# Attention with queries scaled by 1/rms at their layout and the output divided by the sum of the softmax weights

## The chip, the core and the metric

One core of a Trainium2 chip runs the whole program. Its engines work side by side, each through its own queue in order: TensorE (PE, with its weight loads PEld), VectorE (DVE), ScalarE (ACT), GpSimd (POOL), and SyncE (SP), which issues the transfers. The metric is the device time of one execution in microseconds.

## The reference

Two layers of an encoder on 512 tokens of width 1024. Each layer has a mixer, in which attention and a state space part (SSD) share one input and one output projection, and then a feed-forward part (SwiGLU). What matters here is the attention: 8 query heads of 64 and 2 key heads, queries and keys divided by their root mean square (rms) and rotated by position, then, per block of 128 queries, softmax and the weighted sum of the values:

```python
q = rms_norm(q.reshape(b, l, N_Q_HEADS, HEAD_DIM), q_norm_w[i]).astype(jnp.float32)
k = rms_norm(k.reshape(b, l, N_KV_HEADS, HEAD_DIM), k_norm_w[i]).astype(jnp.float32)
...
    def one_block(qi):
        s = jnp.einsum("bqgrd,bkgd->bgrqk", qi, k)
        p = jax.nn.softmax(s, axis=-1)
        return jnp.einsum("bgrqk,bkgd->bqgrd", p, v)
...
    mixed = jnp.concatenate([attn_out, ssd_out], axis=-1)
    x = x + jnp.einsum("ble,ed->bld", mixed, w_out[i])
```

Softmax: with m the largest score of a row, the weights are exp(s - m), divided by their sum.

## The kernel before

Activations lie with features on the partitions, 8 tiles of 128x512; weights come in chunks of 128x1024 floats. Each weight is split into a high and a low part (`whi`, cast on ACT, L188; `wlo`, subtracted on DVE or GpSimd, L189), and so is each operand (`xh`, `xl`); a product is three matmuls (`mm3`, L407 to L409; `mm3a`, L415 to L417).

The mixer of a layer weaves three generators together (`drain`, L926): `fill` (input projections of queries, of x/B/C with their convolution, of z, and then the first half of the output projection), `ssd` (the scan in chunks of 128 tokens) and `att` (attention). A scheduler then sets the order of the instructions on each engine, so that the order in the program is not the one written.

Attention works on 8 blocks, 4 query blocks c for each of 2 key heads g, with 4 query heads j each: 32 pairs of head and block in a layer, 64 in all. `queries` (L646) lays a block out: it copies the 4 heads twice side by side (`qd`, ACT), transposes them on PE and splits them (`qh`, `ql`). `attention` (L659) then does, for each head:

- two matmuls, queries against keys, into the scores `s_` (L664, L665);
- the negated maximum `nm` of each row (L667, DVE), times the query's 1/rms `ri` (L668, DVE);
- `p_` = exp(ri * s_ + nm) with the row sums in `sm` (L670, ACT);
- 1/sm (L671, DVE) and `p_` times it (L675, DVE, 128x512);
- four transposes of `p_` (L678, PE), a copy to SBUF (`t_ring`, ACT);
- after each second head, the product with the values (L688, PE) and the copy of the 128x128 output into `qr` (L690, ACT), in place of the queries.

So the queries are rotated but not divided by their rms when they are laid out: the 1/rms (`qri`, worked out by `rsqrt` on DVE from the sums of squares) comes in at the exponential. The weights are divided before they are used.

At the end of `fill`, `out_half(1, ...)` multiplies the SSD half of the output projection: 8 tiles m of 12 matmuls, each added to `part` (L791, DVE). Then, for j = 0 to 3 (two heads each), the attention's output is split into `mixed.h[j]` (L850, ACT) and `mixed.l[j]` (L851, recorded as xl<-qr,xh L94, DVE). After `drain`, `out_half(0, ...)` multiplies the attention half; its tile m needs all four j. The two halves are called half 1 and half 0 below, in this order of time.

In the SSD part, `chunk` adds the product `yd` to `y` (L766, DVE) before PE may go on to the product with the state (L771); `finish` works out the 1/rms of the SSD half (`yri`) and multiplies `xs` by it (L891).

Of the kernel before, what the change touches and what calls it, by code (L numbers as in the profile page):

```python
# [15 lines left out]
F32 = mybir.dt.float32  # L16
F32R = mybir.dt.float32r
I32 = mybir.dt.int32
AF = mybir.ActivationFunctionType
ALU = mybir.AluOpType  # L20
# [3 lines left out]
P = 128  # L24
# [4 lines left out]
NC = S // P  # L29
# [6 lines left out]
PRODUCTS = "11 c1 c2 22 t3 21 c4".split()  # L36
SRAW = 6

NORM = "VVVV"
PTE = "AAAA"  # L40
GGE = "GG"
QDE, OUTE, _, YE, HE, WE, RAE, MLE, DSE = "AAVGVGVVG"
EB, GGB = 2, 4
DDW, DDE = 512, "A"
MORE = "VGGVG"
# [24 lines left out]
def merge(a, b, c):  # L70
    return a.rearrange("p (b c) -> p b c", b=b, c=c)


def bc(ap, shape, axis):
    return ap.unsqueeze(axis).broadcast_to(shape)
# [3 lines left out]
def tile_hybrid_encoder(ctx, tc, xt_d, par_d, rope_d, snw_d, w_kvdt, w_xbc, w_q, w_z, w_out, w_gate, w_up, w_down, out_d):  # L79
    nc = tc.nc  # L80
    V, A, G, T = nc.vector, nc.scalar, nc.gpsimd, nc.tensor
# [8 lines left out]
    def copy(e, out, in_):  # L90
        A.copy(out, in_) if e == "A" else (G if e == "G" else V).tensor_copy(out, in_)

    def tt(e, *args):
        (G if e == "G" else V).tensor_tensor(*args)  # L94

    def bank(tag):


        return psum.tile([P, S], F32, name=f"ps_{tag}", tag=tag)
# [148 lines left out]
    ident = const.tile([P, P], F32, name="ident")  # L248
# [193 lines left out]
    def mixer(l, norm, mx):  # L442
# [21 lines left out]
        base = mx.tile([P, 2, NC, 64], F32, name="base", tag="t2", bufs=B2)  # L464
# [29 lines left out]
        if l == 0:  # L494
            for t, rows, v in ((segr, (0, 32), 1.0), (segl, (64, 72), -1.0)):
                G.memset(t.bitcast(F32), 0.0)
                for r in rows:
                    G.affine_select(out=t, in_=t.bitcast(F32), pattern=[[-1, 8], [0, P]], compare_op=ALU.not_equal, fill=v,
                                    base=-r, channel_multiplier=1)
# [3 lines left out]
        for d in range(2):  # L503
            for r in (0, 32):
                V.tensor_copy(acw[:, d, :, r:r + 8], ac[:, :, 8 * d:8 * d + 8])
            p_ = bank("m")
            for c in range(NC):
                T.matmul(p_[:64, c * P:(c + 1) * P], lhsT=acw[:, d, c], rhs=mask[("le", "ge")[d]], start=True, stop=True)
            for r in (0, 32):
                dst, src = segl[r:r + 8, 4 * d:4 * d + 4], merge(p_[r:r + 8], NC, P)  # L510
# [50 lines left out]
        for g in range(2):  # L561
            p_ = bank("m")
# [47 lines left out]
        qr = mx.tile([P, NC, 8, 64], F32, name="qr")  # L610
# [17 lines left out]
        qri = {}  # L628
# [13 lines left out]
        def ring(which):  # L642
            turn[which] += 1
            return rings[which][:, turn[which] % 4]

        def queries(c, g):  # L646

            qd = mx.tile([P, 4, 2, 64], F32, name="qd", tag="qd")
            copy(QDE, qd, bc(qr[:, c, 4 * g:4 * g + 4], [P, 4, 2, 64], 2))
            tp = bank("t")  # L650
            for j in range(4):
                T.transpose(tp[:, j * P:(j + 1) * P], qd[:, j].rearrange("p a d -> p (a d)"), ident)
            qh = mx.tile([P, S], F32R, name="qh", tag="qh", bufs=2)
            ql = mx.tile([P, S], F32R, name="ql", tag="ql", bufs=2)
            A.copy(qh, tp)
            V.tensor_tensor(ql, tp, qh.bitcast(F32), ALU.subtract)
            return qh, ql

        def attention(c, g, qh, ql):  # L659
            nm = mx.tile([P, 4], F32, name="nm", tag="nm", bufs=2)  # L660
            sm = mx.tile([P, 4], F32, name="sm", tag="sm", bufs=2)
            for j in range(4):
                s_ = bank("s")
                T.matmul(s_, lhsT=qh[:, j * P:(j + 1) * P], rhs=KK[:, g], start=True, stop=False)  # L664
                T.matmul(s_, lhsT=ql[:, j * P:(j + 1) * P], rhs=KK[:, g], start=False, stop=True)  # L665
                ri = qri[g][:, c, j:j + 1]
                V.tensor_reduce(nm[:, j:j + 1], s_, AX.X, ALU.max, negate=True)  # L667
                V.tensor_tensor(nm[:, j:j + 1], nm[:, j:j + 1], ri, ALU.mult)  # L668
                p_ = ring("p")
                A.activation(p_, s_, AF.Exp, bias=nm[:, j:j + 1], scale=ri, accum_out=sm[:, j:j + 1])  # L670
                V.reciprocal(sm[:, j:j + 1], sm[:, j:j + 1])  # L671
                if NORM[j] == "A":
                    A.activation(p_, p_, AF.Copy, scale=sm[:, j:j + 1])
                else:
                    (G if NORM[j] == "G" else V).tensor_scalar(p_, p_, sm[:, j:j + 1], None, ALU.mult)  # L675
                t_ = bank("t")
                for kt in range(NC):
                    T.transpose(t_[:, kt * P:(kt + 1) * P], p_[:, kt * P:(kt + 1) * P], ident)  # L678
                pt = merge(ring("t"), NC, P)
                copy(PTE[j], pt, merge(t_, NC, P))  # L680
                if j % 2 == 0:
                    first = pt
                    continue
                o_ = bank(O_BANK)

                for kt in range(NC):
                    for e, t2 in enumerate((first, pt)):
                        T.matmul(o_[64 * e:64 * e + 64, :P], lhsT=Vt[:, kt, g * 64:(g + 1) * 64],  # L688
                                 rhs=t2[:, kt], start=kt == 0, stop=kt == NC - 1)
                copy(OUTE, qr[:, c, 4 * g + j - 1:4 * g + j + 1].rearrange("p h d -> p (h d)"), o_[:, :P])  # L690
                yield
# [126 lines left out]
        def fill():  # L818
# [25 lines left out]
            yield from out_half(1, range(KT), part, part)  # L844
            while "att" not in done:
                yield
            for j in range(4):
                src = qr.rearrange("p c (j a) d -> p j c (a d)", a=2)[:, j]
                h = mixed.h[j].rearrange("p (c q) -> p c q", c=NC)
                A.copy(h, src)  # L850
                tt(MLE, mixed.l[j].rearrange("p (c q) -> p c q", c=NC), src, h.bitcast(F32), ALU.subtract)  # L851
            Z["part"] = part

        def drain(*gens):
# [309 lines left out]
```

## Time and profile before

| | us |
|---|---|
| three runs | 1280.83, 1285.01, 1288.04 |
| median | 1285.01 |
| the profiled execution, its own time | 1282.91 |
| its span in the profile | 1281.2 |
| PE, DVE, ACT, POOL busy | 1212.7, 953.1, 618.5, 265.6 |
| mean granted clock of TensorE | 0.977 |

Read it so: PE is busy for nearly the whole span, but matmuls are pipelined, so a busy PE is not one at its peak. The mixers lie at about 20 to 265 us and 645 to 885 us; between and after them is the feed-forward part. Shares over the span mix stages with different limits, so the stages of a mixer are read one by one.

### The profile page before, as it was taken

The numbers are of one execution on the slowest core, as the hardware profiler recorded it, in microseconds if no ns is written. First come the engines' busy times: TensorE is split into PE (matmuls) and PEld (weight loads), VectorE is DVE, ScalarE is ACT, GpSimd is POOL, SyncE is SP. The second block draws the span as 40 slices with busy tenths as digits, with TensorE's granted clock in tenths as the row PEclk, the third lists the DMA queues.
The fourth block names the chain that finished last, engine by engine and source line by source line (L and its number), as shares of the span: only waits on it lengthen the run. The fifth ranks groups of instructions, "written<-read, shape, count | busy, mean of one in ns | idle before, by whom it ended". The sixth has DMA issues, their size and how long they took to land.

```text
span 1281.2 us, 19691 instructions
## 1 busy us (share of the span) xinstructions
PE 1212.7 (95%) x7694; PEld 1072.8 (84%) x7694; DVE 953.1 (74%) x1561; ACT 618.5 (48%) x1131; POOL 265.6 (21%) x208
## 2 busy tenths in 40 slices
PE   6898998999799999999998999899988999999996
PEld 6777887687798999899897787778878889989995
DVE  7899889666874687567679989985597458845853
ACT  4556655543442354244455575754354324523544
POOL 6423655010400000000134255420022000000002
PEclk8999998999899999999999999989999999999998
DMA  5221022125133133221442211112502422332122
GB/s 175 94 71 50 34 67 75 33 93 170 50 116 99 66 129 119 74 71 42 128 141 88 66 34 66 59 34 83 197 17 93 138 72 94 124 119 72 40 61 79
DMA packets 45229, 110.04 MB, mean 86 GB/s; under 512 B 5168, under 2 KB 5680, under 8 KB 45136
## 3 DMA queue, kind: packets, MB, share of 16 engines
q1 hardware_dynamic: 45136, 108.79, 26.4%
q8 instruction: 60, 0.98, 0.3%
q14 instruction: 33, 0.27, 0.1%
HBM read 104.44 MB, written 4.33 MB: 85 GB/s over the span
## 4 chain that ended last, share of the span: by engine, by line
PE 70%; DVE 21%; issue 3%; ACT 2%; POOL 2%; DMA 1%; DVEq 0%; ACTq 0%; POOLq 0%
PE ps_a L1025 5%; PE ps_a L1026 5%; PE ps_a L1024 5%; PE ps_a L1071 3%; PE ps_a L1070 3%; PE ps_a L1072 3%; PE ps_a L407 3%; PE ps_s L1070 3%; PE ps_s L1071 3%; PE ps_s L1072 3%; PE ps_a L408 3%; PE ps_a L409 3%; DVE u L590 3%; PE ps_s L1025 3%; PE ps_s L1024 3%
## 5 line engine op out<-in xcount | busy, mean ns | idle before, releaser
L188 ACT CAST whi<-wraw 128x512 fp32r<-128x512 f32 (+4 forms) x169 | 123.8, 763 | 212.2 <-PE ps_a L408 54.0
L188 ACT CAST whi<-sraw 128x1024 fp32r<-128x1024 f32 x126 | 132.1, 1050 | 181.9 <-PE ps_a L1025 46.6
L189 DVE TENSOR_TENSOR wlo<-sraw,whi 128x1024 fp32r<-128x1024 f32 x126 | 153.9, 1223 | 47.2 <-ACT whi L188 46.7
L319 POOL TENSOR_TENSOR ssq<-ssq,sqt 128x512 f32<-128x512 f32 x17 | 25.9, 1526 | 672.3 <-ACT sqt L316 672.1
L189 DVE TENSOR_TENSOR wlo<-wraw,whi 128x1024 fp32r<-128x1024 f32 (+4 forms) x105 | 107.2, 1032 | 51.2 <-ACT whi L188 50.9
L407 PE MATMUL ps_a<-xh,whi 128*128 128x512 f32 x320 | 126.7, 398 | 3.2 <-DVE a__3069 L967 1.6
L409 PE MATMUL ps_a<-xh,wlo 128*128 128x512 f32 x320 | 126.2, 394 | 0.0
L408 PE MATMUL ps_a<-xl,whi 128*128 128x512 f32 x320 | 126.0, 395 | 0.0
L189 POOL TENSOR_TENSOR wlo<-wraw,whi 128x512 fp32r<-128x512 f32 x64 | 91.1, 1442 | 102.3 <-ACT whi L188 95.2
L163 DVE TENSOR_TENSOR sraw<-sraw 128x1024 f32<-128x1024 f32 x72 | 87.9, 1221 | 1.0
L415 PE MATMUL ps_a<-whi,xh 128*128 128x256 f32 (+1 forms) x256 | 75.6, 298 | 8.2 <-ACT whi L188 8.1
L1024 PE MATMUL ps_a<-ss,whi 128*128 128x256 f32 x288 | 82.0, 285 | 0.0
L1025 PE MATMUL ps_a<-ss,whi 128*128 128x256 f32 x288 | 81.9, 284 | 0.0
L1026 PE MATMUL ps_a<-ss,wlo 128*128 128x256 f32 x288 | 81.9, 284 | 0.0
L1025 PE MATMUL ps_a<-s,whi 128*128 128x256 f32 x288 | 81.1, 283 | 0.0
L1026 PE MATMUL ps_a<-s,wlo 128*128 128x256 f32 x288 | 81.1, 283 | 0.0
L1024 PE MATMUL ps_a<-s,whi 128*128 128x256 f32 x288 | 79.8, 283 | 0.0
L416 PE MATMUL ps_a<-wlo,xh 128*128 128x256 f32 (+1 forms) x256 | 75.6, 296 | 0.3 <-DVE wlo L189 0.2
L407 PEld LDWEIGHTS ps_a<-xh,whi 128*128 128x128 f32 x320 | 60.5, 189 | 17.2 <-ACT s L985 4.0
L417 PE MATMUL ps_a<-whi,xl 128*128 128x256 f32 (+1 forms) x256 | 74.3, 292 | 0.3 <-DVE xl L304 0.3
L409 PEld LDWEIGHTS ps_a<-xh,wlo 128*128 128x128 f32 x320 | 60.4, 189 | 13.3 <-issue 0.8
L408 PEld LDWEIGHTS ps_a<-xl,whi 128*128 128x128 f32 x320 | 60.5, 189 | 12.5 <-DVE xl L805 0.4
(393 smaller groups left out, 3621.0 us busy)
## 6 DMA issues: line engine op xcount, KB each, us to landing
sraw<-in_w_gate SPq DMA_DIRECT2D x72, 256.0 KB, 3.3
sraw<-in_w_up SPq DMA_DIRECT2D x72, 256.0 KB, 3.6
wraw<-in_w_down SPq DMA_DIRECT2D x32, 512.0 KB, 3.6
wraw<-in_w_xbc SPq DMA_DIRECT2D x16, 512.0 KB, 3.2
wraw<-in_w_out SPq DMA_DIRECT2D x16, 512.0 KB, 3.3
wraw<-in_w_down SPq DMA_DIRECT2D x16, 384.0 KB, 3.1
wraw<-in_w_q SPq DMA_DIRECT2D x8, 512.0 KB, 3.3
wraw<-in_w_z SPq DMA_DIRECT2D x8, 512.0 KB, 3.3
```

The source lines that it names most:

```text
L163: V.tensor_tensor(q[to], q[to], q[by], ALU.add)
L188: A.copy(hi[:, u], raw[:, u])
L189: (G if lo_pool else V).tensor_tensor(lo[:, u], raw[:, u], hi[:, u].bitcast(F32), ALU.subtract)
L407: T.matmul(ps, lhsT=wh, rhs=op.h[k], start=first, stop=False)
L408: T.matmul(ps, lhsT=wh, rhs=op.l[k], start=False, stop=False)
L409: T.matmul(ps, lhsT=wl, rhs=op.h[k], start=False, stop=last)
L1024: T.matmul(out, lhsT=wh[:, o:o + P], rhs=x_[:, 0, i], start=first and i + j == 0, stop=False, skip_group_check=True)
L1025: T.matmul(out, lhsT=wh[:, o:o + P], rhs=x_[:, 1, i], start=False, stop=False, skip_group_check=True)
L1026: T.matmul(out, lhsT=wl[:, o:o + P], rhs=x_[:, 0, i], start=False, stop=i == 3, skip_group_check=True)
L1070: T.matmul(ps[:, cols], lhsT=w1[:, o:o + P], rhs=h, start=f == a, stop=False)
L1071: T.matmul(ps[:, cols], lhsT=w1[:, o:o + P], rhs=g, start=False, stop=False)
L1072: T.matmul(ps[:, cols], lhsT=w2[:, o:o + P], rhs=h, start=False, stop=f == b - 1)
```

## The change

Three things. The queries are multiplied by their 1/rms when they are laid out, by four ACT activations with a scale for each block in place of one copy; the maximum and the exponential take the scores as they are. The weights `p_` are not divided; their sums go into one tile `sums` for all heads and blocks. When all attention is done, `normalize` works out 1/sums (one DVE instruction of 128x32), transposes it on PE (four transposes to 8 rows), copies the rows (ACT), and for each j spreads two rows over 128 partitions by a matmul with a selection matrix of zeros and ones (`sel`, filled by GpSimd); DVE multiplies the outputs `qr` by the result out of PSUM, and the split into `mixed.h[j]` and `mixed.l[j]` follows.

```diff
--- before.py
+++ after.py
@@ -36,10 +36,9 @@
 PRODUCTS = "11 c1 c2 22 t3 21 c4".split()
 SRAW = 6
 
-NORM = "VVVV"
 PTE = "AAAA"
 GGE = "GG"
-QDE, OUTE, _, YE, HE, WE, RAE, MLE, DSE = "AAVGVGVVG"
+OUTE, _, YE, HE, WE, RAE, MLE, DSE = "AVGVGVVG"
 EB, GGB = 2, 4
 DDW, DDE = 512, "A"
 MORE = "VGGVG"
@@ -646,7 +645,8 @@
         def queries(c, g):
 
             qd = mx.tile([P, 4, 2, 64], F32, name="qd", tag="qd")
-            copy(QDE, qd, bc(qr[:, c, 4 * g:4 * g + 4], [P, 4, 2, 64], 2))
+            for j in range(4):
+                A.activation(qd[:, j], bc(qr[:, c, 4 * g + j], [P, 2, 64], 1), AF.Copy, scale=qri[g][:, c, j:j + 1])
             tp = bank("t")
             for j in range(4):
                 T.transpose(tp[:, j * P:(j + 1) * P], qd[:, j].rearrange("p a d -> p (a d)"), ident)
@@ -656,23 +656,41 @@
             V.tensor_tensor(ql, tp, qh.bitcast(F32), ALU.subtract)
             return qh, ql
 
+        sums = mx.tile([P, NC, 8], F32, name="sums")
+
+        def normalize():
+
+
+            sel = ring("p")[:8]
+            G.memset(sel, 0.0)
+            pick = merge(sel, 8, 64)
+            G.affine_select(out=pick, in_=pick, pattern=[[-1, 8], [0, 64]], compare_op=ALU.not_equal, fill=1.0,
+                            base=0, channel_multiplier=1)
+            rec = mx.tile([P, NC, 8], F32, name="rec")
+            V.reciprocal(rec, sums)
+            tp = bank("t")
+            for c in range(NC):
+                T.transpose(tp[:8, c * P:(c + 1) * P], rec[:, c], ident)
+            rows = ring("p")[:8]
+            A.copy(rows, tp[:8])
+            for j in range(4):
+                b = bank("s")
+                T.matmul(b, lhsT=sel[:, j * P:(j + 1) * P], rhs=rows, start=True, stop=True)
+                o = qr.rearrange("p c (j a) d -> p j c (a d)", a=2)[:, j]
+                V.tensor_tensor(o, o, merge(b, NC, P), ALU.mult)
+                h = merge(mixed.h[j], NC, P)
+                A.copy(h, o)
+                tt(MLE, merge(mixed.l[j], NC, P), o, h.bitcast(F32), ALU.subtract)
+
         def attention(c, g, qh, ql):
             nm = mx.tile([P, 4], F32, name="nm", tag="nm", bufs=2)
-            sm = mx.tile([P, 4], F32, name="sm", tag="sm", bufs=2)
             for j in range(4):
                 s_ = bank("s")
                 T.matmul(s_, lhsT=qh[:, j * P:(j + 1) * P], rhs=KK[:, g], start=True, stop=False)
                 T.matmul(s_, lhsT=ql[:, j * P:(j + 1) * P], rhs=KK[:, g], start=False, stop=True)
-                ri = qri[g][:, c, j:j + 1]
                 V.tensor_reduce(nm[:, j:j + 1], s_, AX.X, ALU.max, negate=True)
-                V.tensor_tensor(nm[:, j:j + 1], nm[:, j:j + 1], ri, ALU.mult)
                 p_ = ring("p")
-                A.activation(p_, s_, AF.Exp, bias=nm[:, j:j + 1], scale=ri, accum_out=sm[:, j:j + 1])
-                V.reciprocal(sm[:, j:j + 1], sm[:, j:j + 1])
-                if NORM[j] == "A":
-                    A.activation(p_, p_, AF.Copy, scale=sm[:, j:j + 1])
-                else:
-                    (G if NORM[j] == "G" else V).tensor_scalar(p_, p_, sm[:, j:j + 1], None, ALU.mult)
+                A.activation(p_, s_, AF.Exp, bias=nm[:, j:j + 1], accum_out=sums[:, c, 4 * g + j:4 * g + j + 1])
                 t_ = bank("t")
                 for kt in range(NC):
                     T.transpose(t_[:, kt * P:(kt + 1) * P], p_[:, kt * P:(kt + 1) * P], ident)
@@ -844,11 +862,7 @@
             yield from out_half(1, range(KT), part, part)
             while "att" not in done:
                 yield
-            for j in range(4):
-                src = qr.rearrange("p c (j a) d -> p j c (a d)", a=2)[:, j]
-                h = mixed.h[j].rearrange("p (c q) -> p c q", c=NC)
-                A.copy(h, src)
-                tt(MLE, mixed.l[j].rearrange("p (c q) -> p c q", c=NC), src, h.bitcast(F32), ALU.subtract)
+            normalize()
             Z["part"] = part
 
         def drain(*gens):
```

Where it moves instructions. On DVE, early in the mixer of layer 0, where the convolution taps (`u`, from `raw` and `cwh`) and the first softmax rows share the queue. Before:

```order
L667 TENSOR_REDUCE nm<-ps_s 128x1
L590 SCALAR_TENSOR_TENSOR u<-raw,cwh,u 128x512
L668 TENSOR_TENSOR nm<-nm,qri_716 128x1
L671 RECIPROCAL sm<-sm 128x1
L590 SCALAR_TENSOR_TENSOR u<-raw,cwh,u 128x512
L675 TENSOR_SCALAR p_ring<-p_ring,sm 128x512
L582 TENSOR_TENSOR raw<-ps_a,rbc 128x512
```

And now:

```order
L593 SCALAR_TENSOR_TENSOR CT<-th,u 128x512
L589 SCALAR_TENSOR_TENSOR u<-raw,cwh,u 128x512
L691 TENSOR_REDUCE nm<-ps_s 128x1
L589 SCALAR_TENSOR_TENSOR u<-raw,cwh,u 128x512
L691 TENSOR_REDUCE nm<-ps_s 128x1
L589 SCALAR_TENSOR_TENSOR u<-raw,cwh,u 128x512 x2
```

The products with `qri`, the reciprocals and the divisions of `p_ring` are gone from between the taps; the maxima stay.

On DVE in layer 0 ahead of the addition to `y` that PE waits for. Before:

```order
L886 TENSOR_SCALAR ym<-ym 128x4
L668 TENSOR_TENSOR nm<-nm,qri_1729 128x1
L94 TENSOR_TENSOR xl_2775<-qr,xh_2773 128x512 x2
L668 TENSOR_TENSOR nm<-nm,qri_1729 128x1
L281 TENSOR_SCALAR yri0i<-ym 128x4
L766 TENSOR_TENSOR y<-y,ps_m 128x512
```

And now:

```order
L284 TENSOR_TENSOR yri0t<-yri_2230 128x4
L285 TENSOR_TENSOR yri0t<-yri0t,ym 128x4
L286 SCALAR_TENSOR_TENSOR yri_2230<-yri0t,yri_2230 128x4
L905 SCALAR_TENSOR_TENSOR xs<-xs,yri_2230,snw 128x256 x4
L833 SCALAR_TENSOR_TENSOR gz_2042<-zth,gz_2042 128x256
L784 TENSOR_TENSOR y<-y,ps_m 128x512
```

Both splits of the output (`xl` from `qr`) are gone from there; nearly all steps of `yri` (ten rows more of it stand ahead of the six shown) and the products of `xs` with it, which stood behind `y`, stand ahead of it.

On PE in layer 0 where half 1 of the output projection ends and half 0 begins (in the names, `xh`/`xl` of 2297 or 2251 are the SSD half, of 2773 or 2709 the attention half). Before:

```order
L688 MATMUL ps_t<-t_ring,Vt 64x128 x7
L407 MATMUL ps_a<-xh_2297,whi 128x512
L408 MATMUL ps_a<-xl_2299,whi 128x512
L409 MATMUL ps_a<-xh_2297,wlo 128x512
L407 MATMUL ps_a<-xh_2773,whi 128x512
L408 MATMUL ps_a<-xl_2775,whi 128x512
L409 MATMUL ps_a<-xh_2773,wlo 128x512
```

Before, the last output product (L688) is followed by 48 matmuls of half 1 (the three shown, 16 times), and those at once by half 0. And now:

```order
L408 MATMUL ps_a<-xh_2251,wlo 128x512
L706 MATMUL ps_t<-t_ring,Vt 64x128 x7
L673 MATMUL ps_t<-ident,rec 8x128 x4
L678 MATMUL ps_s<-p_ring 128x512 x3
L406 MATMUL ps_a<-xh_2709,whi 128x512 x2
L678 MATMUL ps_s<-p_ring 128x512
L407 MATMUL ps_a<-xl_2711,whi 128x512
L408 MATMUL ps_a<-xh_2709,wlo 128x512
```

The last output product has moved behind all of half 1, the transposes of the reciprocals and the products with the selection matrix follow it, and half 0 starts behind three of these.

## Rows read from the trace of the kernel before

**Rows 1.** The page of the profile, its part 1 (busy time of each engine, share of the span, instructions) and the first line of its part 4 (the chain that ended last, share of the span by engine).

```profile
PE 1212.7 (95%) x7694; PEld 1072.8 (84%) x7694; DVE 953.1 (74%) x1561; ACT 618.5 (48%) x1131; POOL 265.6 (21%) x208
...
PE 70%; DVE 21%; issue 3%; ACT 2%; POOL 2%; DMA 1%; DVEq 0%; ACTq 0%; POOLq 0%
```

**Rows 2.** Busy time in six stretches of the span: the three stages of the mixer of layer 0, then those of layer 1. Columns: stretch, its length, busy us (and instructions begun) of PE, PEld, DVE, ACT, POOL, then the granted clock of TensorE, the share of the DMA engines, GB/s.

```profile
60.00:130.00 70.00, 63.46 (x362) 52.61 (x363) 69.07 (x142) 41.75 (x95) 20.10 (x16) 0.95 0.19 63
130.00:200.00 70.00, 67.46 (x517) 58.69 (x515) 59.01 (x134) 43.65 (x115) 42.46 (x38) 1.00 0.15 46
200.00:245.00 45.00, 38.79 (x255) 30.25 (x255) 36.59 (x96) 27.06 (x69) 13.65 (x12) 0.92 0.16 54
680.00:750.00 70.00, 63.54 (x353) 51.50 (x352) 67.59 (x138) 40.49 (x93) 24.09 (x19) 0.95 0.21 70
750.00:820.00 70.00, 68.57 (x511) 58.79 (x508) 59.98 (x138) 45.14 (x121) 41.44 (x37) 1.00 0.15 46
820.00:865.00 45.00, 40.13 (x276) 32.05 (x274) 39.64 (x97) 27.28 (x69) 14.74 (x13) 0.92 0.17 54
```

**Rows 3.** The chain of waits between 60 and 130 us, by line, in shares of that stretch.

```profile
by line: DVE u L590 25.2%; issue 6.7%; DVE gg L753 5.6%; DVE xsT L600 5.5%; DVE p_ring L675 5.5%; DVE nm L667 5.3%; DVE wlo L189 3.6%; DVE raw L582 3.5%; PE ps_a L416 3.1%; DVE ql L656 2.9%; PE ps_a L415 2.7%; DVE CT L594 2.6%; PE ps_a L417
```

**Rows 4.** All instructions of line 675: shortest, median and longest in ns, first and last start in us.

```profile
L675 DVE TENSOR_SCALAR p_ring<-p_ring,sm x64: 475/486/1602, 89.8 to 860.7; 128x512 f32<-128x512 f32 x64
```

**Rows 5.** The six stretches of rows 2, the instructions of line 675 alone (the division of the softmax weights on DVE). Columns: stretch, its length, busy us of DVE (and instructions), clock, DMA share, GB/s.

```profile
60.00:130.00 70.00, 6.70 (x8) 0.95 0.19 63
130.00:200.00 70.00, 9.66 (x13) 1.00 0.15 46
200.00:245.00 45.00, 6.00 (x12) 0.92 0.16 54
680.00:750.00 70.00, 5.04 (x7) 0.95 0.21 70
750.00:820.00 70.00, 7.79 (x14) 1.00 0.15 46
820.00:865.00 45.00, 6.65 (x12) 0.92 0.17 54
```

**Rows 6.** Instructions of DVE in order of time, at 230 us: start us, duration us, line, operation, operands.

```profile
230.65 0.15 DVE L671 RECIPROCAL sm<-sm 128x1 f32<-128x1 f32 x1
230.72 0.14 DVE L668 TENSOR_TENSOR nm<-nm,qri 128x1 f32<-128x1 f32 x1
230.78 0.15 DVE L286 TENSOR_TENSOR yri2t<-yri2t,ym 128x4 f32<-128x4 f32 x1
```

**Rows 7.** Instructions in order of time at the two places where PE waits for y: start us, duration us, engine, line, operation, operands; in brackets the idle time before and what ended it.

```profile
204.49 5.83 POOL L189 TENSOR_TENSOR wlo<-wraw,whi 128x512 fp32r<-128x512 f32 x4 [4.64 <-ACT whi L188]
...
205.77 3.44 DVE L94 TENSOR_TENSOR xl<-qr,xh 128x512 fp32r<-128x512 f32 x2
...
211.06 1.67 PE L771 MATMUL ps_m<-H,CT 128*128 128x256 f32 x4 [4.24 <-DVE y L766]
...
825.73 1.76 DVE L94 TENSOR_TENSOR xl<-qr,xh 128x512 fp32r<-128x512 f32 x1
...
829.18 1.22 DVE L286 TENSOR_TENSOR yri0t<-yri0t,ym 128x4 f32<-128x4 f32 x1
...
832.32 1.70 PE L771 MATMUL ps_m<-H,CT 128*128 128x256 f32 x4 [3.63 <-DVE y L766]
```

**Rows 8.** Busy time in single microseconds after those two places; the columns are those of rows 2, and the granted clock (1.00 is 2.4 GHz, 0.50 is 1.2 GHz) is the third number from the end.

```profile
212.00:213.00 1.00, 1.00 (x4) 0.30 (x3) 0.39 (x3) 0.00 (x0) 0.83 (x1) 0.50 0.00 0
217.00:218.00 1.00, 1.00 (x3) 0.83 (x3) 1.00 (x5) 0.27 (x1) 0.38 (x1) 0.50 0.00 0
833.00:834.00 1.00, 1.00 (x5) 0.82 (x3) 1.00 (x3) 0.00 (x0) 0.59 (x1) 0.50 0.00 0
838.00:839.00 1.00, 1.00 (x4) 0.81 (x4) 1.00 (x2) 0.59 (x1) 0.42 (x1) 0.50 0.69 279
```

**Rows 9.** The chain of waits, pieces at 245 us, at 249 us and at 305 us: start us, us on the chain, engine, operand, line, instructions.

```profile
244.93 0.44 PE ps_t L678 x4
...
249.13 0.23 PE ps_a L409
...
305.49 0.86 PE ps_m L340 x2
```

**Rows 10.** Instructions in order of time while half 1 of the output projection runs out, between 252 and 264 us.

```profile
252.74 0.62 ACT L850 CAST xh<-qr 128x512 fp32r<-128x512 f32 x1
...
253.40 0.69 DVE L94 TENSOR_TENSOR xl<-qr,xh 128x512 fp32r<-128x512 f32 x1
...
263.32 1.14 ACT L188 CAST whi<-wraw 128x512 fp32r<-128x512 f32 x2 [4.30 <-PE ps_a L408]
...
263.55 0.69 DVE L791 TENSOR_TENSOR part<-part,ps_a 128x512 f32<-128x512 f32 x1 [2.03 <-PE ps_a L409]
```

**Rows 11.** Groups of ACT's instructions by line and shape: operands, count | busy us, mean ns of one | idle time before them and what ended it.

```profile
L91 ACT COPY qd<-qr 128x512 f32<-128x512 f32 x16 | 10.1, 630 | 4.6 <-DVE qr L94 3.5 <-DVE raw L581 1.0
L91 ACT COPY qr<-ps_t 128x128 f32<-128x128 f32 x32 | 8.5, 267 | 13.6 <-PE ps_t L688 13.2
L617 ACT ACTIVATE qr<-ps_a,rtok 128x256 f32<-128x256 f32 x12 | 5.8, 483 | 1.4 <-PE ps_a L417 1.4
L342 ACT COPY rbc<-ps_m 128x512 f32<-128x512 f32 x4 | 2.4, 590 | 6.3 <-PE ps_m L340 6.3
```

## The prediction

> **What bounds the kernel now.** I read the page first, then busy time by stage, then the chain of waits in those stages, then single instructions. TensorE (PE) is busy 95% of the span and carries 70% of the chain, VectorE (DVE) 21% [rows 1]: the feed-forward parts are TensorE's, and the order of their instructions is the same in both kernels, so I leave them alone. The change lives in the two mixers, about 60 to 245 us and 680 to 865 us. I cut each into three stages [rows 2]. Stage A (first 70 us): DVE is busy 69.07 and 67.59 of 70 us, PE 63.5. DVE sets the pace; the chain there is mostly DVE's convolution taps (u L590, 25.2%) with the softmax's p_ring L675 at 5.5% [rows 3]. Stage B (next 70 us): PE 67.46 and 68.57, DVE only 59 to 60. PE sets the pace. Stage C (last 45 us): neither is full (PE 38.79 and 40.13, DVE 36.59 and 39.64), and the clock falls: there is one stall in each layer, below.
>
> **What the change takes from DVE.** For each of 64 (head, query block) pairs three DVE instructions go: the division of the 512 weights (L675), the product of max and 1/rms (L668), the reciprocal (L671). L675 is 0.49 us in the median but up to 1.60 us [rows 4]; the stages have 6.70, 9.66, 6.00 us and 5.04, 7.79, 6.65 us of it [rows 5], 41.8 us in all. The two small ones show 0.15 us, but their starts lie 0.07 us apart in a full queue (230.65, 230.72, 230.78 us) [rows 6]; I count 0.07 us.
>
> Stage A: DVE is the pace, so what leaves its queue leaves the time, up to the next limit. 6.70 + 5.04 us of L675 and 2 layers x 8 pairs x 2 x 0.07 = 2.2 us make 13.9 us. PE's 63.5 of 70 us stands behind it with 6.5 us a layer to spare, and its matmuls wait for DVE too, so I take **11 us**; bounds 5 (PE and ScalarE take over at once) and 14.
>
> Stage B: PE is the pace. What DVE gives up can at most fill PE's idle 2.5 + 1.4 = 4 us [rows 2]; **4 us**, bounds 0 and 4. A pair's path also loses hops (max, product, exp, reciprocal, division, transpose becomes max, exp, transpose), but a chain that is not last gives nothing; this is inside the bound.
>
> Stage C: here both layers have a stall of PE: it waits 4.24 us at 211.06 and 3.63 us at 832.32 for y L766 [rows 7]. Ahead of y in DVE's queue stand subtractions xl<-qr,xh (a pair of 3.44 us in layer 0; one of 1.76 us in layer 1), slow while GpSimd runs (5.83 us of wlo at 204.49). The clock then drops: granted 0.50, that is 1.2 GHz, from 212 to 218 and from 833 to 839 us [rows 8], some 6.5 us at half speed, half of them lost. Stall and low clock: 4.24 + 3.63 + 2 x 3.2 = 14.3 us. The change moves all xl<-qr,xh out of this place, and no division is left between. But the order puts another chain ahead of y: the 1/rms of the SSD half (yri) and four xs products. So I take half, **7 us**; bounds 0 and 14.
>
> On that place a rule of the Trainium skill speaks against the gain. The rows first: with GpSimd running, the tiny product yri0t L286 (128x4) takes 1.22 us, where it takes 0.15 elsewhere [rows 6, 7]. "GPSIMD Engine Reference", Key points, says that GpSimd shares its SBUF interfaces with VectorE, with contention for instructions in a two-port mode or with two SBUF inputs. The trace agrees (L675 0.475 to 1.602 us). By it the yri chain, all of two SBUF inputs, would be as slow as the xl that left, stage C would give 0, and the sum would be 7 us less; that is the first rival.
>
> **What it adds.** The tail: the output's division now stands between the two halves of the output projection. Before, half 1 runs into half 0 without a gap on PE, since the last heads' split (L850 and xl) is done in the shadow of half 1 (xl at 253.40, half 1 ends near 264 us) [rows 10]. Now PE has at that boundary four transposes of rec, four products with the selection matrix, and only then half 0's first matmul. Nothing of PE's own hides them: the order has them after half 1's last matmul. Per layer: transposes 0.44 us (as p_ring's four at 244.93); four 512-column fp32 products at 0.86 us (as L340, two passes) = 3.44 us [rows 9]; and the ScalarE copy of the rows in between. ScalarE first has the cast of the last weight chunk, which in the trace starts as half 1 ends (263.32, 1.14 us), then the 0.27 us copy of the last output, then the rows (0.59, as L342) [rows 10, 11]. From the end of half 1 that is 1.14 + 0.27 + 0.59 = 2.0 us, less 0.2 since the cast starts a little early, against 0.45 (last output products, there before too) + 0.44 on PE: 0.9 us of idle PE. 0.44 + 0.9 + 3.44 = 4.8 us, **9.6 us** for both layers. After that DVE (0.69 a product out of PSUM, as part L791, and 0.69 a split) needs 1.4 us for each of four j and PE six matmuls of 0.23, 1.38 us, and PE has a lead of products to do; so I add nothing. Bounds: below, the bare PE work, 3.9 a layer (7.8); above, all in a row, 0.44 + 0.59 + 0.86 + 4 x (0.69 + 0.62 + 0.69) = 9.9 a layer (19.8). I take the value by PE's rows since the order interleaves the four.
>
> Other edits. The layout of the queries becomes four scaled ScalarE activations of 128x128 for one copy of 0.63 us. No row has that form; the nearest are 0.27 us (128x128 copy out of PSUM, L91) and 0.48 (128x256 with a scale, L617) [rows 11]. At 0.27 it is 1.08, so 0.45 us x 16 = 7 us more of ScalarE; at 0.48 it is 21 us. ScalarE is busy 42 to 45 of 70 us [rows 2] and the layout is done one block ahead: 0, with 7 as the upper end. Its wait for 1/rms is no new one in the code (a block isn't begun before it). GpSimd's fill and select of 8x512 run in the tail, where it has no other work: 0. Two of the four splits of the output per layer leave DVE's busy stage C (counted there).
>
> **Sum.** -11 - 4 - 7 + 9.6 = -12.4 us against the profiled execution's own 1282.91 us: 1270.5. The median of the three runs, 1285.01, lies 2.1 above it: **1273 us**.
>
> **Rivals.** (1) PE takes over and the stall stays: GpSimd slows the yri chain as it did xl, y is as late, the clock falls as before, and stage B, whose PE is full, gives nothing. -11 + 9.6 = -1.4: 1284 us, within 0.5%. For it: the slow 128x4 rows; against: xl and the divisions ahead of y are gone.
> (2) The tail decides: rows, product, cast, split of each j come one after the other on ScalarE, PE and DVE, 9.9 us a layer, with stages B and C giving nothing: -11 + 19.8 = +8.8, **1294 us**, slower. It decides from 5.5 us a layer on (11 / 2) if only stage A gives, from 11 if all do (22 / 2). For it: every link is a wait between engines, and a wait of PE of some 4 us has cost the clock in this trace; against: the order lets PE do three of the products while the first j is split, and the k = 0 matmuls of two banks are issued together.
> (3) All of it: 13.9 + 4 + 14.3 - 7.8 = 24.4 us less, 1261 us. For it: DVE is 97 to 99% busy in stage A, and both stalls end at a DVE instruction; against: the yri chain before y.
> That the instructions would still be there is no case: they are absent from the order.
>
> **How the numbers follow.** Forecast (1266 to 1279) 0.43; rival 1 (1279 to 1290) 0.25; rival 2 (1290 to 1303) 0.17; rival 3 (1255 to 1266) 0.15. The range is 1259 to 1290: it leaves out nearly all of rival 2 and a little of rival 3. What a measurement can tell from no change is about 0.5%, 6.4 us, so faster means under 1278.6 and slower over 1291.4: faster 0.43 + 0.15 less 0.01 for the forecast's upper edge = 0.57, same 0.25 and that edge with a little of rival 2's lower edge, 0.27, slower 0.16.
>
> **What would show it.** In the profile after: 64 max reductions and no p_ring row on DVE; stage A shorter by some 5 us a layer with DVE still near full; no wait of PE for y over 2 us, and no second at clock 0.50 after it; at the end of half 1 four selection products on PE with some 1 us of idle ahead of them and half 0 behind them without gaps. I am wrong if the tail holds more than 6 us of PE between the halves, if stage A keeps its length (another DVE wait, or ScalarE's exp, comes last), or if the low clock moves to another place instead of going.

## The result, and the profile after

The changed kernel takes 1292.56 us in the median of 9 runs (1288.70 to 1294.38), the kernel before 1283.15 (1280.83 to 1288.04, 9 runs): a ratio of 1.0065, 95% interval 1.0047 to 1.0083. It is slower, where I had forecast 1273 and faster. The profiled execution after has a span of 1290.5 us against 1281.2.

The first part of the page after, and the first line of its part 4, as in [rows 1]:

```profile
PE 1225.6 (95%) x7718; PEld 1077.8 (84%) x7718; DVE 911.4 (71%) x1379; ACT 624.6 (48%) x1181; POOL 265.8 (21%) x212
...
PE 72%; DVE 17%; ACT 3%; POOL 3%; issue 3%; DMA 1%; DVEq 0%; ACTq 0%; POOLq 0%
```

DVE has 41.7 us less to do, about the 41.8 us of divisions that are gone; PE is busy 12.9 us longer with only 24 matmuls more. The six stretches, with the columns of [rows 2]:

```profile
60.00:130.00 70.00, 66.61 (x402) 55.16 (x403) 61.79 (x121) 48.12 (x117) 25.64 (x20) 0.98 0.20 63
130.00:200.00 70.00, 67.68 (x503) 59.14 (x501) 53.25 (x107) 44.87 (x126) 38.87 (x35) 0.98 0.17 50
200.00:245.00 45.00, 39.98 (x253) 31.75 (x252) 27.53 (x52) 22.09 (x58) 13.32 (x14) 0.92 0.18 59
680.00:750.00 70.00, 65.00 (x348) 52.61 (x347) 64.80 (x123) 42.38 (x97) 27.49 (x21) 0.95 0.24 77
750.00:820.00 70.00, 69.30 (x531) 61.42 (x530) 54.07 (x100) 47.29 (x143) 41.10 (x37) 1.00 0.15 46
820.00:865.00 45.00, 39.81 (x276) 32.17 (x275) 31.22 (x67) 27.06 (x71) 15.14 (x15) 0.96 0.16 53
```

In the first 70 us of each mixer DVE is no longer full, and PE does more. In the last 45 us DVE has 8 to 9 us less to do than before, yet PE is hardly busier, and its clock still dips to a mean of 0.92 in layer 0 (0.96 in layer 1, where it was 0.92). The stretches hold other work now, so I follow four landmarks instead: the last state addition (DVE, into `H`), the eighth addition into `part` (half 1 is done), the last addition into `x` (half 0 is done), and the first convolution tap of layer 1. Times in us are those at which the instruction starts, in layer 1 counted from that first tap (674.88 before, 680.74 after); the last row runs from the start of the eighth addition to the end of the last one into `x`:

| | layer 0 before, after | change | layer 1 before, after | change | forecast, both |
|---|---|---|---|---|---|
| last state addition (stages A, B) | 165.47, 157.93 | -7.5 | 115.0, 107.2 | -7.8 | -15 |
| half 1 done (stage C after it) | 263.55, 256.42 | -7.1 | 209.6, 202.3 | -7.2 | -22 |
| from there to half 0 done | 22.45, 34.53 | +12.1 | 22.45, 32.99 | +10.5 | +9.6 |

Up to the end of half 1 that is 14.3 us less, behind it 22.6 us more, and 0.9 us more ahead of layer 1's first tap: 9.2 of the 9.3 us between the spans.

The place where half 1 ends, in order of time, columns as in [rows 7]:

```profile
256.42 0.69 DVE L809 TENSOR_TENSOR part<-part,ps_a 128x512 f32<-128x512 f32 x1 [2.62 <-PE ps_a L408]
...
257.33 0.60 PE L673 MATMUL ps_t<-ident,rec 128*8 128x128 f32 x4
...
257.97 0.57 ACT L675 COPY p_ring<-ps_t 8x512 f32<-8x512 f32 x1 [0.27 <-PE ps_t L673]
...
258.69 3.94 PE L678 MATMUL ps_s<-p_ring 8*128 8x512 f32 x6 [0.76 <-ACT p_ring L675]
...
263.71 2.07 PE L678 MATMUL ps_s<-p_ring 8*128 8x512 f32 x2
...
272.86 1.29 DVE L809 TENSOR_TENSOR x<-part,ps_a 128x512 f32<-128x512 f32 x2 [4.92 <-PE ps_a L408]
```

The transposes, the rows and the idle of 0.76 us stand as forecast. But the fourth product (two passes, the x2 row) takes 2.07 us for 0.86, and the first two tiles of half 0 are added only at 272.86. Single microseconds there, the clock third from the end as in [rows 8]:

```profile
259.00:260.00 1.00, 1.00 (x3) 0.37 (x2) 0.18 (x1) 0.00 (x0) 0.00 (x0) 1.00 0.64 168
260.00:261.00 1.00, 1.00 (x3) 0.44 (x2) 0.68 (x2) 0.46 (x1) 0.00 (x0) 0.68 0.89 356
261.00:262.00 1.00, 1.00 (x2) 0.06 (x1) 1.00 (x2) 0.60 (x2) 0.00 (x0) 0.50 0.00 0
...
269.00:270.00 1.00, 1.00 (x4) 0.81 (x3) 0.00 (x0) 0.00 (x0) 0.00 (x0) 0.50 0.00 0
270.00:271.00 1.00, 1.00 (x4) 0.76 (x4) 0.00 (x0) 0.00 (x0) 0.00 (x0) 0.70 0.00 0
```

From 259 us on PE is shown busy throughout, and its clock is 1.2 GHz for some 10 us, from the middle of the selection products on. Layer 1 has the same for some 7 us, from 888.4 to 895.2 us, again ahead of the fourth product. This is nowhere in my prediction.

The other place is stage C, where [rows 7] had the wait for y:

```profile
198.70 0.16 DVE L286 SCALAR_TENSOR_TENSOR yri<-yri0t,yri 128x4 f32<-128x4 f32 x1
...
198.94 5.14 POOL L188 TENSOR_TENSOR wlo<-wraw,whi 128x512 fp32r<-128x512 f32 x4 [3.44 <-ACT whi L187]
199.09 1.14 DVE L285 TENSOR_TENSOR yri0t<-yri0t,ym 128x4 f32<-128x4 f32 x1
200.27 1.20 DVE L286 SCALAR_TENSOR_TENSOR yri<-yri0t,yri 128x4 f32<-128x4 f32 x1
201.50 4.66 DVE L905 SCALAR_TENSOR_TENSOR xs<-xs,yri,snw 128x256 f32<-128x256 f32 x4
...
206.42 0.68 DVE L784 TENSOR_TENSOR y<-y,ps_m 128x512 f32<-128x512 f32 x1
...
207.15 2.07 PE L789 MATMUL ps_m<-H,CT 128*128 128x256 f32 x4 [4.33 <-DVE y L784]
```

The wait of PE for y is 4.33 us, as long as before, behind other instructions: a step of the yri chain takes 0.16 us until GpSimd begins the four wlo, and 1.14 to 1.20 us beside them. In layer 1 PE waits 3.59 us at 834.17. In both layers the clock is low again behind the wait: 0.50 from 206 to 212 us and from 834 to 837 us. A stretch of layer 0, with the columns of [rows 2]:

```profile
205.00:210.00 5.00, 2.85 (x8) 2.29 (x8) 3.98 (x7) 0.00 (x0) 1.75 (x2) 0.57 0.00 2
```

### The profile page after: what moved, and what is told of

The parts are those of the page before. It is cut to its first block, busy times and chain, and to the rows that moved or that the text cites. A ratio compares the mean times of both kernels' runs of the same rounds, so it can differ in the third digit from the quotient of the medians.

```text
span 1290.5 us, 19613 instructions
## 1 busy us (share of the span) xinstructions
PE 1225.6 (95%) x7718; PEld 1077.8 (84%) x7718; DVE 911.4 (71%) x1379; ACT 624.6 (48%) x1181; POOL 265.8 (21%) x212
## 3 DMA queue, kind: packets, MB, share of 16 engines
HBM read 104.44 MB, written 4.33 MB: 84 GB/s over the span
## 4 chain that ended last, share of the span: by engine, by line
PE 72%; DVE 17%; ACT 3%; POOL 3%; issue 3%; DMA 1%; DVEq 0%; ACTq 0%; POOLq 0%
PE ps_a L1040 5%; PE ps_a L1039 5%; PE ps_a L1038 5%; PE ps_a L406 4%; PE ps_a L407 4%; PE ps_a L408 4%; PE ps_a L1084 3%; PE ps_a L1085 3%; PE ps_a L1086 3%; PE ps_s L1084 3%; PE ps_s L1086 3%; PE ps_s L1085 3%; PE ps_s L1040 3%; PE ps_s L1039 3%; PE ps_s L1038 3%
## 5 line engine op out<-in xcount | busy, mean ns | idle before, releaser
L407 PE MATMUL ps_a<-xl,whi 128*128 128x512 f32 x320 | 128.7, 403 | 0.0
L406 PEld LDWEIGHTS ps_a<-xh,whi 128*128 128x128 f32 x320 | 61.8, 194 | 22.6 <-ACT s L999 4.0
```

The costliest lines, as they stand in the source:

```text
L406: T.matmul(ps, lhsT=wh, rhs=op.h[k], start=first, stop=False)
L407: T.matmul(ps, lhsT=wh, rhs=op.l[k], start=False, stop=False)
```

## The experiments

Each ran beside runs of the kernel before; ratios are to those. Three questions: what drops the clock between the halves, what keeps the wait for y, and which half of the change does what.

**Rows padded.** The selection matrix and the rows get 128 partitions in place of 8, the rest zeros:

```diff
-            sel = ring("p")[:8]
+            sel = ring("p")
...
-            rows = ring("p")[:8]
-            A.copy(rows, tp[:8])
+            rows = ring("p")
+            G.memset(rows, 0.0)
+            A.copy(rows[:8], tp[:8])
```

> The changed kernel with the selection matrix and the reciprocal rows padded with zeros from 8 to 128 rows, so that the four selection products of a layer use all 128 rows of the array; same count, same result, and GpSimd fills one more 128x512 tile. Theory A (the products with 8 rows are what drops the clock: in the profile after it is granted 1.00 up to 260 us and 0.50 from 261 to 270 us, with PE shown busy): the clock stays at 1.00 in the tail of both layers, which gives back half of some 9.7 and 6.6 us at half speed, 8 us: 1284 us, the same as before the change. Rival B (PE's gap of 0.76 us for the copied rows and its waits for DVE between the products drop it, the number of rows does not matter): the clock falls in the same place and the time is that of the changed kernel, 1290 to 1294.

1283.55 us, ratio 0.9999 (0.9986 to 1.0011): 9 us back. In order of time, with the gap ahead of the products as it was, and then two single microseconds:

```profile
256.57 0.69 DVE L810 TENSOR_TENSOR part<-part,ps_a 128x512 f32<-128x512 f32 x1 [2.62 <-PE ps_a L408]
...
258.80 3.03 PE L679 MATMUL ps_s<-p_ring 128*128 128x512 f32 x6 [0.72 <-ACT p_ring L676]
...
262.13 1.02 PE L679 MATMUL ps_s<-p_ring 128*128 128x512 f32 x2
...
267.75 1.28 DVE L810 TENSOR_TENSOR x<-part,ps_a 128x512 f32<-128x512 f32 x2 [2.41 <-PE ps_a L408]
```

```profile
262.00:263.00 1.00, 1.00 (x5) 0.47 (x4) 1.00 (x3) 0.37 (x2) 0.00 (x0) 1.00 0.06 16
266.00:267.00 1.00, 1.00 (x6) 0.84 (x5) 0.00 (x0) 0.00 (x0) 0.00 (x0) 1.00 0.00 0
```

The clock stays at 1.00 in both layers. From half 1's end to half 0's it is 29.26 us in both, against 34.53 and 32.99: 5.3 + 3.7 = 9.0 us, the whole difference of the two times. Theory A holds, rival B falls: the gap is there and drops nothing.

**The gap hidden, the rows not padded.** The counterpart: half 1 in two parts with the normalisation between.

```diff
-            yield from out_half(1, range(KT), part, part)
+            yield from out_half(1, range(4), part, part)
             while "att" not in done:
                 yield
             normalize()
+            yield from out_half(1, range(4, KT), part, part)
```

> The changed kernel with half 1 written in two parts and the normalisation between them, so that the transposes of the reciprocals and the copy of the rows lie under the last 12 matmuls of half 1; the selection products keep their 8 rows and follow half 1 without a gap. Theory A (8-row products drop the clock, the idle 0.76 us ahead of them does not): the clock still falls to 0.50 in the tail of both layers, only the idle comes back, 1289 to 1293 us. Rival B (the gap drops it): the clock stays at 1.00 there, 1281 to 1285.

1291.50 us, ratio 1.0052 (1.0037 to 1.0067). The products now follow half 1 without idle (their row carries no wait); then single microseconds:

```profile
255.02 3.64 PE L678 MATMUL ps_s<-p_ring 8*128 8x512 f32 x6
```

```profile
255.00:256.00 1.00, 1.00 (x4) 0.49 (x4) 0.87 (x2) 1.00 (x2) 0.00 (x0) 1.00 0.00 0
256.00:257.00 1.00, 1.00 (x3) 0.17 (x1) 1.00 (x3) 0.04 (x1) 0.00 (x0) 1.00 0.03 8
257.00:258.00 1.00, 0.93 (x2) 0.29 (x2) 1.00 (x3) 0.62 (x1) 0.00 (x0) 0.79 0.00 0
258.00:259.00 1.00, 1.00 (x2) 0.41 (x2) 1.00 (x3) 0.62 (x1) 0.00 (x0) 0.50 0.38 102
...
266.00:267.00 1.00, 1.00 (x3) 0.75 (x3) 0.00 (x0) 0.00 (x0) 0.00 (x0) 0.50 0.00 0
```

The clock falls all the same. So the two runs together show that it is the products over 8 rows, not a gap of PE. Only 8 and 128 rows were run: from how many rows on the clock holds isn't known.

**No division.** The outputs are split as in the kernel before and never divided by the sums (that part is left out), `normalize()` being replaced by the four lines it had taken the place of.

> The changed kernel without its division: the outputs are split as in the kernel before and are not divided by the sums (that part of the computation is left out). It prices the whole tail. Theory A (tail 11 to 12 us a layer instead of the predicted 4.8, while the mixer up to the end of half 1 gained 7 us a layer): 1292.6 less 21 to 23, about 1270 us, with PE running from half 1 into half 0 without a gap. By the prediction's own tail (9.6 us) it would be 1283. If the last heads' copies, which now end only with half 1, hold up half 0 by themselves, some 1275 to 1280.

1272.10 us, ratio 0.9909 (0.9894 to 0.9924). From half 1's end to half 0's it takes 24.31 us in both layers:

```profile
255.36 1.09 PE L706 MATMUL ps_t<-t_ring,Vt 128*64 128x128 f32 x14
255.47 0.69 DVE L809 TENSOR_TENSOR part<-part,ps_a 128x512 f32<-128x512 f32 x1 [2.63 <-PE ps_a L408]
...
261.70 1.29 DVE L809 TENSOR_TENSOR x<-part,ps_a 128x512 f32<-128x512 f32 x2 [3.57 <-PE ps_a L408]
...
262.44 0.50 PE L406 MATMUL ps_a<-xh,whi 128*128 128x512 f32 x1 [0.33 <-DVE x L809]
...
279.09 0.69 DVE L809 TENSOR_TENSOR x<-part,ps_a 128x512 f32<-128x512 f32 x1 [0.58 <-PE ps_a L408]
```

That prices the tail in three parts, for each layer: 24.31 - 22.45 = 1.9 us come without any division, from the new order around the place; 29.26 - 24.31 = 4.95 us are the division at full clock; 5.3 and 3.7 us are the clock. Of the 1.9 us, 1.1 are the last 14 output products (the first row), which stood ahead of the end of half 1 before (1.09 us at 251.32 there): they have only moved across the landmark. Most of the rest comes behind the first two tiles of half 0, which now end together, so that PE waits 0.33 us for their additions. Theory A's 1270 is met within some 2 us.

**The low parts on VectorE.** The wlo of half 1's four weight chunks leaves GpSimd:

```diff
         for i in range(4):
-            stream(w_out[l, 1, i], 1024, 1, 512)
+            stream(w_out[l, 1, i], 1024, 0, 512)
```

> The changed kernel with the low parts of the four weight chunks of half 1 (wlo, eight 128x512 subtractions a layer) made on VectorE in place of GpSimd, so that GpSimd is idle while the yri chain runs. Theory C (the stall for y stays because GpSimd's wlo slows the chain that stands ahead of y: yri steps of 1.14 to 1.20 us and four xs products of 4.66 us, and the low clock follows from the stall): the steps take some 0.15 us, PE's wait for y in stage C falls from 4.33 to under 2 us, the clock stays up there, and 3 to 7 us a layer come back, less what VectorE pays for 8 subtractions of 0.65 us a layer where it is waited for: 1282 to 1289 us. Rival (the place of y in the queue and VectorE's own load decide, whatever GpSimd does): the wait stays over 3.5 us, 1291 to 1297.

1280.56 us, ratio 0.9977 (0.9963 to 0.9992) against 1.0065: 11 us by the ratios, 12 by the medians. In order of time, the same chain in the same order ahead of y:

```profile
197.17 0.16 DVE L286 SCALAR_TENSOR_TENSOR yri<-yri0t,yri 128x4 f32<-128x4 f32 x1
197.25 0.69 DVE L188 TENSOR_TENSOR wlo<-wraw,whi 128x512 fp32r<-128x512 f32 x1
...
197.85 2.69 DVE L905 SCALAR_TENSOR_TENSOR xs<-xs,yri,snw 128x256 f32<-128x256 f32 x4
...
201.07 0.68 DVE L784 TENSOR_TENSOR y<-y,ps_m 128x512 f32<-128x512 f32 x1
...
201.80 1.13 PE L789 MATMUL ps_m<-H,CT 128*128 128x256 f32 x4 [1.39 <-DVE y L784]
```

No step of the chain is over 0.17 us, the four xs take 2.69 us for 4.66, PE waits 1.39 us for 4.33 (1.42 in layer 1), and the clock is 1.00 from 200 to 215 and from 820 to 835 us. Eight subtractions of 0.69 us more on VectorE are less than it gets back. Theory C holds, with more than the 3 to 7 us a layer in layer 0 (half 1 done at 248.61 for 256.42) and 4.1 us in layer 1; the time lies 1.4 us under the range.

**The same move in the kernel before,** the same line, nothing else.

> The kernel before with half 1's wlo on VectorE and nothing else. Theory C (the stalls for y of 4.24 and 3.63 us, and the low clock behind them, are GpSimd's doing in the kernel before too): 1273 to 1279 us, with the wait for y under 2 us. Rival (VectorE, which there still makes all divisions, has no room for eight more subtractions a layer): 1282 to 1288, and then what this move is worth depends on the change having freed VectorE.

1273.23 us, ratio 0.9919 (0.9902 to 0.9935). Before [rows 7], the pair xl<-qr,xh took 3.44 us and PE waited 4.24; now, in order of time:

```profile
198.76 0.68 DVE L94 TENSOR_TENSOR xl<-qr,xh 128x512 fp32r<-128x512 f32 x1
...
199.44 0.68 DVE L94 TENSOR_TENSOR xl<-qr,xh 128x512 fp32r<-128x512 f32 x1
...
203.00 0.67 DVE L766 TENSOR_TENSOR y<-y,ps_m 128x512 f32<-128x512 f32 x1
...
203.73 1.13 PE L771 MATMUL ps_m<-H,CT 128*128 128x256 f32 x4 [0.83 <-DVE y L766]
```

So the stall was GpSimd's doing in the kernel before as well, and curing it needs nothing of the change: VectorE had room without it. The rival falls.

**Both cures on the changed kernel** (rows padded, wlo on VectorE).

> Both cures at once on the changed kernel: rows padded to 128 and half 1's wlo on VectorE. If the two causes are separate (the stall for y, worth 12 us here, and the clock of the tail, worth 9): 1292.6 - 12.0 - 9.0 = 1271.6, taken as 1269 to 1275 us. If one hides the other, or the clock falls elsewhere once more: over 1276.

1271.63 us, ratio 0.9902 (0.9883 to 0.9922). The two gains add up as forecast: the causes are separate.

**The halves of the change.** First the queries scaled at their layout alone (`queries`, the maximum and the exponential as after; reciprocal, division and split as before).

> Only the first part of the change: queries scaled by 1/rms at their layout, the maximum and the exponential taken as they are; the weights are divided head by head as before, and there is no tail. Theory A (the gain ahead of the tail comes from the 512-column divisions that left VectorE, 41.8 us of it, and the 128x1 products are worth little): 1279 to 1284 us. Rival (the shorter path from the maximum to the exponential is worth as much as the divisions): under 1278. If the four scaled copies on ScalarE cost: over 1287.

1278.57 us, ratio 0.9959 (0.9945 to 0.9972). It gains 5.3 us by the ratio although the 41.8 us of divisions are all still there, so the 128x1 products, the shorter path or the order that comes with them are worth more than I thought; the time lies between the two expectations, and the run doesn't separate the three. Its wait for y is the longest of all, 5.70 us at 204.96 and 6.25 at 829.28. Then the sums alone (`qd` one copy, 1/rms in maximum and exponential as before).

> Only the second part: the queries are laid out by one copy as before and 1/rms enters at the maximum and the exponential; the output is divided by the sums in the tail. Theory A: as the whole change, 1290 to 1295 us, with the tail as long as there (16 to 17 us from the eighth add into part to the second add of half 0). Rival (the 64 small products ahead of the exponential are what counts): over 1297.

1289.39 us, ratio 1.0040 (1.0025 to 1.0055). That is 0.6 us under its range, with a tail 1.4 us shorter in layer 0 than in the whole change: the first add of half 0 comes 15.0 us after the eighth into `part`, for 16.4. The interval overlaps that of the whole change: on top of the sums the scaling gives nothing that can be told. Where its 5 us went can be seen in the traces, one of each kernel (here the fastest execution, 1285.95 us). The whole change is 5.1 us ahead of the sums alone at the last state addition of layer 0 (157.93 for 163.02) and 4.5 us behind at the end of half 1 (256.42 for 251.97); in layer 1 it is 6.5 us ahead at the first landmark and level at the second. It loses its lead in stage C. With the sums alone GpSimd still makes wlo there and yri steps still take 1.19 to 1.22 us, but PE has four products to do between two shorter waits, and its clock is 1.00 from 200 to 216 and from 822 to 838 us:

```profile
201.40 1.13 PE L790 MATMUL ps_m<-H,CT 128*128 128x256 f32 x4 [2.34 <-DVE ee L764]
...
205.21 1.13 PE L790 MATMUL ps_m<-H,CT 128*128 128x256 f32 x4 [1.77 <-DVE y L785]
```

So the order decides too, whether the slow chain makes one long wait with a low clock behind it. That this is so in the other executions of this kernel is not shown.

**Queries scaled, wlo on VectorE.**

> Queries scaled at their layout, weights divided head by head (no tail), and the low parts of half 1's weights made on VectorE. Theory C: as in the run before it, against 1278.6 us for the same kernel with wlo on GpSimd, where PE waits 5.70 us for y in layer 0: 1268 to 1275. Rival (VectorE, which still divides the weights, has no room for 5 us of subtractions a layer): 1279 to 1286.

1271.48 us, ratio 0.9909 (0.9893 to 0.9924), 6 to 7 us under the same kernel with wlo on GpSimd: theory C again, with waits for y of 1.02 and 0.93 us. But it can't be told from the kernel before with that move (0.9919).

**Three tries at hiding the tail.** The normalisation in two parts, the first key head's as soon as its four blocks are done:

```diff
                 yield from attention(c, g, *now)
+                if i + 1 == NC:
+                    normalize(0)
...
-            normalize()
+            normalize(1)
```

> The normalisation in two parts, with rows padded to 128: the heads of the first key head are divided as soon as their four blocks are done, inside the mixer, and only two selection products and two divisions are left between half 1 and half 0. Theory A (what is left of the tail at full clock, about 5 us a layer, is half products on PE and half waits for the copied rows and the first divided j): half 0 starts on the two j that are ready, the tail falls by some 3 us a layer, and the moved products cost at most their 1.7 us a layer in stage B: 1277 to 1281 against 1283.6 with the padding alone. Rival (it only moves PE work into a stage where PE is full, and VectorE's added work there delays y): 1283 to 1288.

1290.38 us, ratio 1.0054 (1.0040 to 1.0069), 7 us worse than the padding alone. The clock holds there, but attention ends later: two heads' transposes, at 258.04 and 261.30, have fallen behind half 1, PE is busy only 8.20 of the 10 us from 260 to 270, and the first add of half 0 comes 13.4 us after half 1's last. The rival's direction holds, 2.4 us above its range and by a chain that it did not name.

Then half 1 in two parts as above, padded, with a raised scheduling priority for the last two blocks and the normalisation:

> The padded kernel with half 1 written in two parts, the normalisation between them, and the scheduler's priority raised for the last two blocks' transposes, outputs and the normalisation, so that the rows are copied and the first j divided under half 1's last matmuls. Theory A (the four products of 0.86 us are PE's own and stay; the 0.7 us of idle and the interleaving are hidden): 1279 to 1282 against 1283.6. Rival (the raised priority delays the SSD chain or half 1's own casts by as much): 1283 to 1288.

1291.41 us, ratio 1.0067 (1.0051 to 1.0082). Here the rows are copied at 255.75, five us ahead of the products, and the gap is gone; half 1 itself ends at 263.59 (products of the division stand ahead of its end), 7.0 us later than with the padding alone, and what lies behind it is only 3.9 us shorter (25.35 for 29.26); the wait for y is 4.33 us still. The rival's direction holds, 3.4 us above its range.

At last all three without the priority: padded, wlo on VectorE, half 1 in two parts.

> All three: rows padded, half 1's wlo on VectorE, and the normalisation written into half 1 so that the rows are copied under its last matmuls. If the idle of some 0.7 us a layer and the first divided j can be hidden: 1 to 3 us less than without the last step, 1267 to 1272. If what remains is the four products of 0.86 us on PE and the chain of division, cast and split behind them: no difference to the run before the last, 1270 to 1275.

1269.59 us (1268.21 to 1271.00), ratio 0.9887 (0.9871 to 0.9903), the fastest of all. Against the same without the split of half 1 the gain of 2.0 us is the size expected, but the intervals overlap. Against the kernel before with wlo on VectorE, timed on the same chip (1271.83 to 1275.77), it is 3.6 us less by the medians, and the runs of the two don't overlap: that is what the change is worth with its tail padded and partly hidden and the stall for y cured in both.

## Why the prediction was wrong, step by step

**Stages A and B: right in sum, by luck in part.** 11 + 4 = 15 us were forecast, 15.3 measured at the last state addition. The split between the stages was off: at the last convolution tap only 4.7 and 1.9 us had been gained. And the cause given isn't borne out: 11.7 of the 13.9 us of stage A were divisions that leave VectorE's queue, and the shorter path of a pair was to give nothing. With the sums alone, where divisions and reciprocals are gone, the last state addition comes only 2.5 and 1.3 us earlier than before; with the scaling alone, all divisions still there, 8.4 and 2.6. These are single traces (four of kernels that differ from the whole change only behind that point, or not at all, spread over 1.3 us there), and the parts don't add up in layer 1; how the 15 us divide is not shown.

**Stage C: wrong.** "So I take half, 7 us": it gave nothing, 15.3 us of gain became 14.3, and 2.2 of these are the output products that moved behind the landmark. What I named as rival 1's mechanism held there: yri steps of 1.2 us beside GpSimd, y as late, the clock low after it. I had the row that said so (the 128x4 product of 1.22 us in [rows 7]) and gave it 0.25. "GPSIMD Engine Reference", Key points, of the Trainium skill has the rule (shared SBUF interfaces, contention for VectorE instructions with two SBUF inputs); the trace agrees, 0.16 against 1.14 to 1.20 us, and moving wlo away takes the slow steps away with it. The step that failed is the reading of the stall as one of "what stands ahead of y": it was one of what ran beside it, and this change, which exchanges the instructions ahead of y, left it (the sums alone, with another order, split it in two). The prediction's "all of two SBUF inputs" was a misreading besides: the chain has steps with one, and before, one of them (L282, a tensor and a constant) took 1.21 us beside wlo at 824.54.

**The tail: its links right, its clock missing.** 4.8 us a layer were forecast for transposes, idle and products; the division at full clock costs 4.95. But the sum priced PE's work at 0.86 us a product and took half 0 behind it at 0.23 a matmul, both rows at full clock, and in the changed kernel the clock falls to 1.2 GHz in the middle of the products and stays there for some 10 and 7 us: 9.0 us for both layers, a term that the sum did not have. And 1.9 us a layer come from the new order around it, which I had at nothing: I took the last output products as "there before too", at 0.45 us, and they take 1.09 and had stood ahead of half 1's end. 9.6 became 22.6.

**Rival 2** gave 1294 us and so nearly the time, but not for its reason: it had the four links of each j in a row, 9.9 us a layer, and the padded run shows 4.95 with the same links. I had weighed that "a wait of PE of some 4 us has cost the clock in this trace", and looked for waits alone; there was none here.

**ScalarE** at 0: no sign of the contrary. With the queries scaled alone, where the four activations stand without the tail, the kernel is faster.

**Sum.** Forecast -22 + 9.6 = -12.4; measured -14.3 + 22.6 + 0.9 = +9.2. Of the 21.6 us between them, 9.0 are the clock of the tail, 7.7 the gain missing at the end of half 1, which stage C was to give, 3.7 the new order, 0.3 the division itself, and 0.9 lie ahead of layer 1's first tap.

What stays open: what of the gain of the scaling alone is the products, what the path and what the order; how the 15 us ahead of stage C divide; and whether the sums alone keep the clock in stage C in their other executions too.

## What to carry to other kernels

Price a matmul that is put into a dense stream not only by its own time: look at how many rows of the array it uses, and give the clock of all that follows it a term of its own; padding the operands with zeros costs little and shows at once whether that is the cause. When an engine is late at a place, ask what runs beside its instructions before counting what stands ahead of them: moving the neighbour alone was worth some 11 us here, on the changed kernel and on the one before. And test such a cure on the old kernel too, since its gain needn't belong to the change.

## What the runs showed of the hardware that I had not expected

Products over 8 rows (eight passes of 512 columns a layer) took the clock from 1.00 to 0.50 before they were done, while PE was shown busy in every microsecond behind their start (0.93 in one), with a gap ahead of them and without; the same passes over 128 rows, 120 of them zeros, left it at 1.00. At full clock the two forms take the same time: six passes 2.99 us over 8 rows (885.35 us, layer 1) and 3.03 over 128.

Beside GpSimd's two-input subtraction a 128x4 instruction of VectorE took 1.14 to 1.20 us for 0.16, four 128x256 products 4.66 for 1.67 (after, 831.84 us, with GpSimd idle; the 2.69 above still has another product of GpSimd beside it), a pair of 128x512 subtractions 3.44 for 1.36. Each slow instruction is about as long as one of GpSimd's subtractions beside it (1.3 us in the changed kernel, 1.5 before), the 128x512 ones a little longer. So the small ones lose most in proportion, sevenfold, and here a chain of them is where GpSimd's help cost more than it saved.
